# A written VectorE order for the opening of the feed-forward stream, and ordering edges behind ScalarE's copies of partial sums in the second layer

## The chip, the cores and the metric

One core of a Trainium2 chip runs the whole kernel in one launch. The metric is device time in microseconds, the median of several executions. TensorE (PE) multiplies, VectorE (DVE), ScalarE (ACT) and GpSimd (POOL) work element by element, SyncE (SP) issues the transfers. Each engine takes its instructions strictly in the order in which they stand in its queue; engines wait for one another by semaphores.

## The reference, cut to what matters

Two layers run over 1024 latent tokens and 256 context tokens. The change touches only the second half of a layer, the feed-forward block with a hidden width of 2816:

```
h2 = rms_norm(xl, norm_ffn) * (1 + sc2) + sh2
xl = xl + g2 * ((silu(h2 @ w_gate) * (h2 @ w_up)) @ w_down)
```

The first layer does this for the context tokens too (`has_ctx` in the kernel), the second for the latent tokens alone. Every float32 operand of a matrix product is split into two float16 parts, a high and a low one, and each product is the sum of three float16 products (high·high, high·low, low·high).

## The kernel before

The hidden width is cut into 22 columns of 128. Columns 0 and 1 are computed plainly, in what is called the opening here: `first_ffn` and the lines behind `wod()` multiply their gate and up weights with `h2` into the PSUM tiles `Sg` and `Su` (and `Sg1`, `Su1` for the first 512 tokens of column 1), ACT applies Silu into `sg`, and DVE multiplies `Su` into it. Those matmuls stand at L1415 and L466.

The other columns go in pairs through the stream (`steps`, from L1673). Each job is one weight block (gate, up or down) of 2x2 pieces times an activation block of 2x2 pieces, done with seven products instead of eight. The products are named "1" to "7"; each is 12 matmuls of 128x512 in a gate or up job and 6 in a down job, all at L1910. Product "1" uses piece B11 of the activations, "2" B21, "3" B22, "4" T4, "5" T1, "6" T2, "7" T3. B11 and B21 are parts of `h2` itself. T1, T2 and T3 are sums and differences of its blocks, which `h_ops` (L1518) makes once for each layer: for each of four slices k, three additions of high and low parts into tiles `rb` (two on POOL, one on DVE), three subtractions on DVE, one subtraction into the scratch `scv` from which T4 comes, and three splits into the tiles `tq` (high part on ACT, low part on DVE). In the first layer products "c0", "c1" and "c2" (L1922, PSUM tile `dx`) multiply the context tokens.

On the weight side POOL forms sums `ws` of staged blocks (`st`, `raw`), and `piece_ahead` (L1716) splits the pieces into the tile `hlp`, ACT the high part and DVE the low one. There is room for four pieces of a gate or up job ahead of PE.

Each job owns three PSUM banks, `Swb`, `Swc` and `Swa`; two sets take turns. Bank b takes product "1", then "6", "5" and "3" on top. After "1", "6" and "5" the running sum has to be taken out before the next one may be added, which `copy` (L1808) does on ACT, into one of four parts of `scv` (named `T` in the profile). `consume` (L1820) does what follows each product, and puts later work into `late` with a step number (`defer`, L1814), which `run_late` (L1925) runs after that step. `t_ops` (L1576) turns two finished columns into the seven operands of the next down job.

The written order of these calls sets a priority; a scheduler then places each instruction on its engine's queue, and may let one pass another where nothing binds them. Before the first product of the stream the tiles `Sg` and `Su` have to be read, since `split_banks` gives their PSUM to the stream's banks.

All activations are issued by one helper (L152), scalar_tensor_tensor by another (L166), tensor_tensor by a third (L169). In the changed kernel these lines are L175, L96 and L195 (every DVE operation has L96 there).

Of the kernel before, what the change touches and what calls it, by code (L numbers as in the profile page):

```python
# [81 lines left out]
def hybrid_kernel(ctx: ExitStack, tc: tile.TileContext, I, out, dbg=None):  # L82
    nc = tc.nc
    V, S, G, TE, DMA = nc.vector, nc.scalar, nc.gpsimd, nc.tensor, nc.sync
# [51 lines left out]
    order = mybir.DependencyInfo(mybir.DependencyClass.NoSync, mybir.DependencyReason.DATA)  # L136
# [12 lines left out]
    def act(o, i, f=AF.Copy, **kw):  # L149
        if f in (AF.Exp, AF.Ln) and tabs["kind"] != "el":  # L150
            preload()
        b = S.activation(o, i, f, **kw).ins  # L152
        if f in (AF.Exp, AF.Ln):
            after(b, tabs["pre"])
            tabs["last"] = tabs["last"][-7:] + [b]
        elif f in (AF.Tanh, AF.Silu):
# [6 lines left out]
            tabs["last"] = [b]  # L163

# [576 lines left out]
    for l in range(DEPTH):  # L741
# [776 lines left out]
        def h_ops():  # L1518
# [20 lines left out]
        wod()  # L1539
        wt = w_get(("gate", l, 1)), w_get(("up", l, 1), False)  # L1540
        sgs = [pt_((P, NTOK), F32, "pf", PFB, "sg") for _ in range(2)]
        pre = [bank("Sg1"), bank("Su1")]

        for k in range(4):
            tt(scv[:, k], h2[:, 4 + k, 0, H0], h2[:, 4 + k, 1, H0], ADD, G)
        for t0 in (512, 768):
            drain(nt[t0])
            for w, S_ in ((f0["wg"], f0["Sg"]), (f0["wu"], f0["Su"])):
                for _ in fm_steps(S_[:, t0:t0 + 256], w, h2, t0, 256):
                    pass  # L1550
                pump(2)
        sg, Sg, Su = sgs[0], f0.pop("Sg"), f0.pop("Su")
        f0.clear()
        act(sg[:, :NTq], Sg[:, :NTq], AF.Silu, scale=INV)
        stt(sg[:, :NTq], Su[:, :NTq], 1.0 / SW, sg[:, :NTq], MUL, MUL)
        spawn(h_ops())
        for w, S_ in zip(wt, pre):
            for _ in fm_steps(S_, w, h2, 0, 512):
                pump()
        act(sgs[1][:, H0], pre[0], AF.Silu, scale=INV)  # L1560
        stt(sgs[1][:, H0], pre[1], 1.0 / SW, sgs[1][:, H0], MUL, MUL)
        pre = None
        sg, Sg, Su = sgs[1], bank3("Sg"), bank3("Su")
        for w, S_ in zip(wt, (Sg, Su)):
            for (t0, n) in blks[1:]:
                fm(S_[:, t0:t0 + n], w, h2, t0, n)
                pump()
# [447 lines left out]
```

## Time and profile before

| | us |
|---|---|
| median of 3 executions | 2798.6 (2792.37 to 2801.43) |
| the profiled execution | 2797.35 |
| its span, first to last instruction | 2795.6 |
| opening of the first layer's stream | about 718 to 762 |
| first layer's stream | 762 to 1485 and a little beyond |
| opening of the second layer's stream | about 2144 to 2191 |
| second layer's stream | 2191 to 2752 |

Times in the rows are microseconds from the span's start. A row of the timeline has start, length, engine, line, operation, output and inputs, count, and in brackets how long the engine had been idle before it and whose end released it. A row of the groups has the count, the busy time, the mean in ns and the idle time before with its releasers. PE is the engine that is nearly always busy, so only its gaps, and what ended them, are time that can be had.

### The profile page before, as it was taken

What the parts mean: (1) busy time and instruction counts of PE and PEld (TensorE: products, weight loads), DVE (VectorE), ACT (ScalarE), POOL (GpSimd) and SP (SyncE); (2) the same over time, 40 slices, a digit from 0 to 9 for tenths busy, and PEclk for the clock granted to TensorE, in tenths of its full rate; (3) what the DMA queues carried; (4) which work ended last, traced back from release to release, by engine and by line L of the source; (5) the groups of instructions that cost most, each with busy time, mean ns of one, the idle gap of its engine ahead of it and who ended that gap; (6) DMA issues with size and microseconds to landing.
All of it is one profiled execution on the core that took longest, in us unless ns stands there. A gap on an engine that the chain in (4) does not pass through costs nothing. (4 is left out here: it accounts for less than half of the span.)

```text
span 2795.6 us, 53695 instructions
## 1 busy us (share of the span) xinstructions
PE 2568.2 (92%) x21403; PEld 1504.1 (54%) x21403; DVE 1882.3 (67%) x3217; ACT 1388.2 (50%) x2650; POOL 1283.8 (46%) x979
## 2 busy tenths in 40 slices
PE   7999989987799999999999998988878799999997
PEld 4875556655455555555555674545555344444444
DVE  5458867778756655656566558866788667576666
ACT  5345557775443434434344445466764444444353
POOL 1124446774434434444443213456764555555641
PEclk9999999999899999999999999999989899999999
DMA  9544499995123222232212222499982121211211
GB/s 299 143 122 113 127 203 186 196 178 116 52 84 91 77 90 83 85 90 77 69 38 78 69 62 69 122 187 180 194 172 69 46 61 53 61 54 53 61 53 76
DMA packets 631632, 296.23 MB, mean 106 GB/s; under 512 B 362888, under 2 KB 620756, under 8 KB 630868
## 3 DMA queue, kind: packets, MB, share of 16 engines
q1 hardware_dynamic: 631204, 292.73, 42.9%
q8 instruction: 167, 2.74, 0.4%
q14 instruction: 85, 0.70, 0.1%
q10 hardware_dynamic: 176, 0.07, 0.0%
HBM read 176.19 MB, written 20.87 MB: 70 GB/s over the span
## 5 line engine op out<-in xcount | busy, mean ns | idle before, releaser
L1910 PEld LDWEIGHTS <-hlp 128*128 128x128 f16 x5040 | 492.4, 98 | 607.5 <-issue 32.8
L1910 PE MATMUL Swb<-T,hlp 128*128 128x512 f16 x1920 | 445.2, 382 | 29.7 <-ACT T L152 14.0
L169 POOL TENSOR_TENSOR phl<-pf,phl 128x1280 f16<-128x1280 f32 (+1 forms) x132 | 345.3, 2618 | 173.7 <-ACT phl L152 115.8
L166 DVE SCALAR_TENSOR_TENSOR hlp<-ws,hlp 128x512 f16<-128x512 f32 (+1 forms) x320 | 231.5, 730 | 146.8 <-ACT hlp L152 119.8
L152 ACT ACTIVATE hlp<-ws 128x512 f16<-128x512 f32 (+1 forms) x320 | 163.6, 518 | 221.8 <-PE Swb L1910 89.3
L152 ACT ACTIVATE pf<-Sp,mx,rq 128x1280 f32<-128x1280 f32 (+1 forms) x144 | 189.6, 1318 | 117.2 <-DVE mx L1320 101.0
L1315 DVE TENSOR_REDUCE mx<-Sp 128x1 f32<-128x1280 f32 (+1 forms) x132 | 194.9, 1477 | 64.3 <-PE Sp L1311 57.2
L1910 PE MATMUL Swc<-T,hlp 128*128 128x512 f16 x960 | 227.2, 379 | 0.0
L1910 PE MATMUL Swb<-tq,hlp 128*128 128x512 f16 x960 | 220.5, 379 | 3.7 <-ACT T L152 3.7
L1374 PE MATMUL pwo<-T,hl 128*128 128x512 f16 (+1 forms) x960 | 194.0, 353 | 32.2 <-DVE X L166 14.4
L466 PE MATMUL pfm<-T,hl 128*128 128x512 f16 (+1 forms) x1032 | 218.1, 365 | 2.6 <-ACT E L152 2.4
L152 ACT ACTIVATE T<-sg 128x512 f16<-128x512 f32 (+1 forms) x170 | 100.3, 600 | 233.4 <-POOL sg L169 155.6
L1311 PE MATMUL Sp<-T 128*128 128x512 f16 (+1 forms) x800 | 171.3, 351 | 41.9 <-ACT pf L152 39.4
L166 DVE SCALAR_TENSOR_TENSOR hlp<-st,hlp 128x256 f16<-128x256 f32 (+1 forms) x201 | 144.2, 721 | 89.0 <-ACT hlp L152 74.1
L169 POOL TENSOR_TENSOR ws<-st 128x256 f32<-128x256 f32 (+1 forms) x97 | 103.9, 1079 | 185.0 <-DMA st<-in_w_ffn_down_dram 70.1
L1922 PE MATMUL dx<-T,hlp 128*128 128x256 f16 x1440 | 178.1, 273 | 11.4 <-DVE hlp L166 6.4
L169 POOL TENSOR_TENSOR X<-X,T 128x512 f32<-128x512 f32 x80 | 112.7, 1408 | 147.0 <-DVE X L166 110.6
L1910 PE MATMUL Swa<-T,hlp 128*128 128x512 f16 x720 | 169.1, 380 | 0.0
L1922 PEld LDWEIGHTS <-hlp 128*128 128x128 f16 x1440 | 139.4, 100 | 43.9 <-issue 9.9
L152 ACT ACTIVATE hlp<-st 128x256 f16<-128x256 f32 (+1 forms) x201 | 101.2, 510 | 110.8 <-PE Swb L1910 72.4
L1374 PEld LDWEIGHTS <-hl 128*128 128x128 f16 x960 | 97.6, 103 | 107.3 <-issue 37.1
L152 ACT ACTIVATE phl<-pf 128x1280 f16<-128x1280 f32 (+1 forms) x115 | 144.5, 1261 | 21.0 <-DMA pT<-phl 18.8
(322 smaller groups left out, 4742.3 us busy)
## 6 DMA issues: line engine op xcount, KB each, us to landing
T<-in_w_ada_dram SPq DMA_DIRECT2D x48, 512.0 KB
rawa<-in_w_ada_dram SPq DMA_DIRECT2D x48, 512.0 KB
st<-in_w_in_dram SPq DMA_DIRECT2D x32, 512.0 KB
st<-in_w_out_dram SPq DMA_DIRECT2D x64, 256.0 KB
st<-in_w_ffn_gate_dram SPq DMA_DIRECT2D x32, 512.0 KB
st<-in_w_ffn_up_dram SPq DMA_DIRECT2D x30, 512.0 KB
st<-in_w_ffn_down_dram SPq DMA_DIRECT2D x30, 512.0 KB
xs<-X SPq DMA_DIRECT2D x4, 2048.0 KB
```

What stands on the lines that cost most here:

```text
L152: b = S.activation(o, i, f, **kw).ins
L166: V.scalar_tensor_tensor(o, a, s, b, op0=o0, op1=o1)
L169: (e or V).tensor_tensor(o, a, b, op=op)
L466: mm(o, w[:, a, k, :], h[:, k, b, t0:t0 + n], start=(k == 0 and j == 0), stop=(k == nk - 1 and j == 2))
L1311: mm(Sp[:, e * nk + b0:e * nk + b0 + m], ql, qkv[:, 4 + h // 4, a, k0 + b0:k0 + b0 + m], start=(a == 0), stop=(a == 1), skip_group_check=True)
L1315: r = V.tensor_reduce(mx[:, :ne], Sp[:, :n].rearrange("p (e k) -> p e k", e=ne), axis=AX.X, op=MAX)
L1374: mm(pb, w[:, a, k, :], mixT[:, k0 + k, b, t0:t0 + n], start=(k == 0 and j == 0), stop=(k == 3 and j == 2))
L1910: mm(o, w[:, a, k, :], B[:, b], start=(s in "172" and k == 0 and j == 0), stop=(k == kh(i) - 1 and j == 2), skip_group_check=True)
L1922: mm(dbank[i][:, r * 256:(r + 1) * 256], w[:, a, k, :], B[:, b], start=(first and k == 0 and j == 0), stop=(not first and k == kh(i) - 1 a ...
```

## The change

DVE gets a wrapper that, while it is switched on, ties each DVE instruction by an ordering edge to the one written before it. An edge of this kind is no semaphore: it binds the scheduler on one engine's queue. It is on from the multiplication of `Su` into the first `sg` until the operands of `h_ops` are made.

`h_ops` does all three additions on DVE, in another sequence, and puts the `scv` subtraction behind the splits. It is no longer one of the threads that are advanced between matmuls; its four slices are called at set places. The whole opening stands behind the definitions of the stream, and the first weight pieces (`prepare()`) are prepared in it, ahead of the last slices of `h_ops`.

The stream's first steps are reordered: "1", "2", "c0", "7", "6" in place of "7", "1", "2", "c0", "6" in the first layer; "1" and "2" of the first job, "1" of the second, then "7", "6", "5" in the second layer, where it was "1", "7", "6", "2", "5".

In the second layer every activation that is written after a copy of a partial sum is tied behind that copy. The copies get six scratch buffers there in place of four in rotation, each given back when its reader has been issued. Late work runs after steps "1", "7", "6" and "4" only, and that of "4" in the same step.

```diff
-    V, S, G, TE, DMA = nc.vector, nc.scalar, nc.gpsimd, nc.tensor, nc.sync
+    row = {"on": False, "last": None}
+    class InRow:
...
+            def call(*a, **k):
+                b = f(*a, **k)
+                if row["on"]:
+                    if row["last"] is not None:
+                        tc.add_manual_dep(b.ins, row["last"].name, order, reason="written order")
+                    row["last"] = b.ins
+                return b
...
+    V = InRow(nc.vector)
...
         b = S.activation(o, i, f, **kw).ins
+        if tabs.get("copy") is not None:
+            tc.add_manual_dep(b, tabs["copy"].name, order, reason="behind the last copy")
...
-                for r, kk, c, e in ((r12, k, H1, G), (r11, k, H0, V), (r22, 4 + k, H1, G)):
-                    tt(r, h2[:, kk, 0, c], h2[:, kk, 1, c], ADD, e)
+                for r, kk, c in ((r22, 4 + k, H1), (r12, k, H1), (r11, k, H0)):
+                    tt(r, h2[:, kk, 0, c], h2[:, kk, 1, c], ADD)
...
-                tt(scv[:, k], scv[:, k], r22, SUB)
                 for op, r in (("T3", r12), ("T2", r22), ("T1", r11)):
                     split2(tpc[op][k], r, V)
+                tt(scv[:, k], scv[:, k], r22, SUB)
...
-            add(0, "7", "1", "2", "c0", "6")
+            add(0, "1", "2", "c0", "7", "6")
...
-            for i in range(nj + 1):
-                add(i, "1", "7")
...
+            add(0, "1", "2")
+            add(1, "1")
+            add(0, "7", "6", "5")
+            for i in range(1, nj + 1):
+                add(i, *("17" if i > 1 else "7"))
...
+        act(sg[:, :NTq], Sg[:, :NTq], AF.Silu, scale=INV)
+        in_row(True)
+        stt(sg[:, :NTq], Su[:, :NTq], 1.0 / SW, sg[:, :NTq], MUL, MUL)
+
+        ho = h_ops()
...
+        act(sg[:, 512:NTq], Sg[:, 512:NTq], AF.Silu, scale=INV)
+        if not last:
+            next(ho)
+        stt(sg[:, 512:NTq], Su[:, 512:NTq], 1.0 / SW, sg[:, 512:NTq], MUL, MUL)
...
+        prepare()
+        for _ in ho:
+            pass
+        drain()
+        in_row(False)
...
+        scs = [scv[:, i] for i in range(4)]
+        if not has_ctx:
+            scs += [T2v[:, o:o + 1024].bitcast(F32) for o in (7168, 15360)]
...
+            b = act(scs[z], src, scale=scale)
+            if not has_ctx:
+                tabs["copy"] = b
...
+                soon = n + (1 if has_ctx or s != "4" else 0)
...
-                    defer(n + 1, fn)
+                    defer(soon, fn)
...
-            run_late(n)
+
+            if has_ctx or s in "1764":
+                run_late(n)
```

What this does to the queues is shown at three places. The first is DVE's queue at the second layer's opening, from the end of the norm (`t`, and `T_72`, which is `h2`); `rb` and `tq` are the tiles of `h_ops`, `T_73` the scratch and the operands of the down jobs. Before:

```order
L166 SCALAR_TENSOR_TENSOR t<-X,prm_142,sq 128x256 x2
L169 TENSOR_TENSOR rb<-T_72 128x512
L166 SCALAR_TENSOR_TENSOR T_72<-t,prm_142,T_72 128x256 x2
L169 TENSOR_TENSOR rb<-rb 128x512
L169 TENSOR_TENSOR rb<-T_72 128x512
L169 TENSOR_TENSOR rb<-rb 128x512 x3
L166 SCALAR_TENSOR_TENSOR sg<-Su,sg 128x1024
L169 TENSOR_TENSOR T_73<-T_73,rb 128x512
L169 TENSOR_TENSOR tq<-rb,tq 128x512 x3
```

The same stretch of DVE's queue in the changed kernel:

```order
L96 SCALAR_TENSOR_TENSOR t<-X,prm_142,sq 128x256 x2
L96 SCALAR_TENSOR_TENSOR T_72<-t,prm_142,T_72 128x256 x2
L96 SCALAR_TENSOR_TENSOR sg<-Su,sg 128x1024
L96 TENSOR_TENSOR rb<-T_72 128x512 x3
L96 TENSOR_TENSOR sg<-sg 128x512
L96 TENSOR_TENSOR rb<-rb 128x512 x2
L96 TENSOR_TENSOR T_73<-sg,T_73 128x512
L96 TENSOR_TENSOR rb<-rb 128x512
L96 TENSOR_TENSOR tq<-rb,tq 128x512 x3
L96 TENSOR_TENSOR T_73<-T_73,rb 128x512
L96 SCALAR_TENSOR_TENSOR sg<-Su_26223,sg 128x512
```

The last writes of `h2` and the read of `Su` now stand ahead of all `rb` work. The read of the last `Su` (`sg<-Su,sg 128x512`) stood behind all four slices of `h_ops`; it now stands behind the second slice, ahead of the third, in the first layer behind the third (`128x768`). POOL's eight `rb<-T_72` additions in each layer are gone from its queue.

The second place is ACT's queue in the second layer's opening; `sg<-Sg` is a Silu, `hlp` a weight piece, `raw` one of the staged weight blocks. Before:

```order
L152 ACTIVATE sg<-Sg 128x1024
L152 ACTIVATE tq<-rb 128x512 x4
L152 ACTIVATE sg<-Sg_26222 128x512
L152 ACTIVATE T_73<-sg 128x512
L152 ACTIVATE hlp<-st 128x512 x2
L152 ACTIVATE tq<-rb 128x512 x6
L152 ACTIVATE hlp<-ws 128x512
L152 ACTIVATE sg<-Sg 128x512
```

The same stretch of ACT's queue in the changed kernel:

```order
L175 ACTIVATE sg<-Sg 128x1024
L175 ACTIVATE hlp<-st 128x512 x2
L175 ACTIVATE T_73<-sg 128x512
L175 ACTIVATE sg<-Sg_26222 128x512
L175 ACTIVATE T_73<-sg 128x512
L175 ACTIVATE tq<-rb 128x512 x3
L175 ACTIVATE hlp<-raw 128x512
L175 ACTIVATE T_73<-sg 128x512
L175 ACTIVATE hlp<-ws 128x512
L175 ACTIVATE tq<-rb 128x512 x2
L175 ACTIVATE sg<-Sg 128x512
L175 ACTIVATE tq<-rb 128x512
```

Three weight pieces moved forward, and one of them, `hlp<-raw`, now stands ahead of the second slice's `tq` and of the last Silu.

The third place is ACT's queue in the second layer's stream, where the first gate job after an up job ends; `T_73<-Swb` is the copy of a partial sum, `T_73<-sg` a split of `t_ops`, `sg<-sg` a Silu. Before:

```order
L152 ACTIVATE hlp<-ws 128x512
L152 ACTIVATE T_73<-sg 128x512
L152 ACTIVATE sg<-sg 128x512
L152 ACTIVATE hlp<-ws 128x512
L152 ACTIVATE T_73<-Swb 128x512
L152 ACTIVATE sg<-sg 128x512
L152 ACTIVATE hlp<-raw 128x512
L152 ACTIVATE T_73<-Swb 128x512
```

The same stretch in the changed kernel:

```order
L175 ACTIVATE hlp<-ws 128x512
L175 ACTIVATE T_73<-sg 128x512
L175 ACTIVATE T_73<-Swb 128x512
L175 ACTIVATE hlp<-ws 128x512
L175 ACTIVATE T_73<-Swb 128x512
L175 ACTIVATE sg<-sg 128x512 x2
L175 ACTIVATE hlp<-raw 128x512
```

Both Silus and one weight piece moved behind the copies; the split of `t_ops` still stands ahead of the first.

## Rows read from the trace of the kernel before

**Rows 1.** Busy time by stretch: stretch, length, PE, PEld, DVE, ACT, POOL, PEclk, DMA, GB/s.

```profile
718.00:762.00 44.00, 29.99 (x178) 16.80 (x177) 39.63 (x49) 18.23 (x32) 25.34 (x16) 0.87 0.13 37
762.00:1485.00 723.00, 723.00 (x4707) 402.26 (x4706) 434.28 (x659) 299.56 (x604) 311.63 (x269) 1.00 0.26 77
2144.00:2191.00 47.00, 28.18 (x122) 12.31 (x120) 42.19 (x50) 19.59 (x33) 26.77 (x17) 0.78 0.11 34
2191.00:2752.00 561.00, 544.08 (x2504) 245.26 (x2504) 366.54 (x529) 252.77 (x491) 297.15 (x251) 1.00 0.18 54
```

**Rows 2.** Who waited for whom, PE, 718 to 762: us, times, longest.

```profile
PE Sg L1415 <- DVE T L166: 2.6, 2, 1.8
```

**Rows 3.** Timeline of PE in the first layer's opening.

```profile
740.11 7.96 PE L466 MATMUL Su<-T,hlr 128*128 128x512 f16 x48
...
760.63 1.46 PE L1922 MATMUL dx<-T,hlp 128*128 128x256 f16 x6 [6.43 <-DVE hlp L166]
761.88 3.79 PE L1910 MATMUL Swc<-tq,hlp 128*128 128x512 f16 x12
...
772.43 2.75 PE L1910 MATMUL Swb<-tq,hlp 128*128 128x512 f16 x12
```

**Rows 4.** Timeline of PE in the second layer's opening.

```profile
2162.24 5.34 PE L466 MATMUL Su<-T,hlr 128*128 128x512 f16 x24
2181.37 1.01 PE L1910 MATMUL Swb<-T,hlp 128*128 128x512 f16 x2 [13.79 <-DVE sg L166]
...
2185.89 4.45 PE L1910 MATMUL Swb<-T,hlp 128*128 128x512 f16 x10 [1.80 <-DVE hlp L166]
2191.18 0.59 PE L1910 MATMUL Swb<-tq,hlp 128*128 128x512 f16 x2 [0.84 <-ACT T L152]
...
2195.92 2.32 PE L1910 MATMUL Swa<-T,hlp 128*128 128x512 f16 x10
2198.08 2.75 PE L1910 MATMUL Swb<-tq,hlp 128*128 128x512 f16 x12
```

**Rows 5.** Timeline of DVE, POOL and ACT in both openings.

```profile
722.72 1.24 ACT L152 ACTIVATE sg<-Sg 128x1280 f32<-128x1280 f32 x1 [2.77 <-PE Sg L1415]
...
724.34 2.48 DVE L169 TENSOR_TENSOR rb<-rb 128x512 f32<-128x512 f32 x4
...
726.75 1.48 DVE L166 SCALAR_TENSOR_TENSOR sg<-Su,sg 128x1280 f32<-128x1280 f32 x1
...
2143.36 4.18 POOL L169 TENSOR_TENSOR rb<-T 128x512 f32<-128x512 f16 x3
...
2143.61 1.64 DVE L169 TENSOR_TENSOR rb<-T 128x512 f32<-128x512 f16 x1
```

**Rows 6.** Timeline of SP and POOL: two weight transfers and one use.

```profile
2162.43 0.37 SPq L370 DMA_DIRECT2D raw<-in_w_ffn_up_dram  x1
...
2185.89 0.37 SPq L370 DMA_DIRECT2D st<-in_w_ffn_up_dram  x1
...
2189.71 1.46 POOL L169 TENSOR_TENSOR ws<-raw,st 128x512 f32<-128x512 f32 x1 [6.24 <-DMA st<-in_w_ffn_up_dram]
```

**Rows 7.** Groups of PE in 2191 to 2752, the two with idle time.

```profile
L1910 PE MATMUL Swb<-T,hlp 128*128 128x512 f16 x948 | 219.3, 381 | 13.9 <-ACT T L152 13.8
...
L1910 PE MATMUL Swb<-tq,hlp 128*128 128x512 f16 x480 | 110.3, 379 | 3.7 <-ACT T L152 3.7
```

**Rows 8.** Timeline of PE: two of the stops of that stream.

```profile
2318.40 2.75 PE L1910 MATMUL Swb<-T,hlp 128*128 128x512 f16 x12 [2.57 <-ACT T L152]
...
2467.87 4.05 PE L1910 MATMUL Swb<-T,hlp 128*128 128x512 f16 x18 [2.24 <-ACT T L152]
```

**Rows 9.** Timeline of ACT ahead of the first of these stops.

```profile
2316.12 0.63 ACT L152 ACTIVATE T<-sg 128x512 f16<-128x512 f32 x1 [2.52 <-DVE sg L169]
...
2316.72 0.63 ACT L152 ACTIVATE sg<-sg 128x512 f32<-128x512 f32 x1
...
2317.77 0.58 ACT L152 ACTIVATE T<-Swb 128x512 f32<-128x512 f32 x1
```

More of the change, by code (lines that the diff above doesn't have):

```diff
@@ L1595, in hybrid_kernel @@
-        if has_ctx:
-            for e in range(2):
-                split2(a_ctx(0, e), sgs[e][:, T:], G)
-        for which in ("C11", "C22", "C12", "C21"):
-            t_ops(0, which)
-        hlt = [wk.tile([P, 2048], F16, tag="hl", name="hlp", bufs=2) for _ in range(2)]
+        hlt = []
         ring = [None] * 8
@@ L1783, in free @@
                     ring[s] = None
+        wod()
+        wt = w_get(("gate", l, 1)), w_get(("up", l, 1), False)
+        sgs = [pt_((P, NTOK), F32, "pf", PFB, "sg") for _ in range(2)]
+        pre = [bank("Sg1"), bank("Su1")]
+        for k in range(4):
+            tt(scv[:, k], h2[:, 4 + k, 0, H0], h2[:, 4 + k, 1, H0], ADD, G)
+        for t0 in (512, 768):
+            drain(nt[t0])
+            for w, S_ in ((f0["wg"], f0["Sg"]), (f0["wu"], f0["Su"])):
+                for _ in fm_steps(S_[:, t0:t0 + 256], w, h2, t0, 256):
+                    pass
+                pump(2)
@@ new lines, in hybrid_kernel, with t_ops @@
+        prepare()
+        for _ in ho:
+            pass
+        drain()
+        in_row(False)
+        for k in range(4):
+            split2(h2[:, k, :, H1], scv[:, k], V)
+        def t_ops(p, which):
+            (p11, p12), (p21, p22) = ((s[:, H0], s[:, H1]) for s in sgs)
+            if which == "C11":
+                split2(a_op(p, "B11"), p11, G)
+            elif which == "C22":
+                split2(a_op(p, "B22"), p22, G)
+            elif which == "C12":
+                tt(p11, p12, p11, SUB)
+                tt(p12, p22, p12, SUB)
+                tt(p22, p22, p11, SUB)
+                split2(a_op(p, "T3"), p12, V)
+                split2(a_op(p, "T2"), p22, V)
+                split2(a_op(p, "T1"), p11, V)
+            else:
+                split2(a_op(p, "B21"), p21, G)
+                tt(p21, p21, p22, SUB)
+                split2(a_op(p, "T4"), p21, V)
@@ L1786, in hybrid_kernel @@
+        if has_ctx:
+            for e in range(2):
+                split2(a_ctx(0, e), sgs[e][:, T:], G)
+        for which in ("C11", "C22", "C12", "C21"):
+            t_ops(0, which)
         adaq = list(range(48)) if l == 0 else []
@@ L1864, in consume @@
                     tt(dst, src, t, ADD)
-                    defer(n + 1, lambda: act(dst, dst, AF.Silu, scale=INV))
+                    end()
+                    defer(soon, lambda: act(dst, dst, AF.Silu, scale=INV))
                 else:
@@ L1870, in fn @@
                         tt(dst, dst, t, MUL, G)
+                        end()
                         if fin:
@@ L1946, in hybrid_kernel @@
         run_late(len(steps) + 9)
+        tabs["copy"] = None
         while pend or adaq:
```

107 lines of the change are left out of this document (40 added, 67 removed).

## The prediction

> **What bounds the kernel now.** I read the busy times by stretch first: PE's row says where time can be had. In the first layer's stream PE is busy for all of its 723.0 us, so nothing done to other engines there shortens it, and whatever the opening ahead of it saves is kept to the end. PE is idle in three stretches that the change touches: 14.0 us of the 44 in the first opening, 18.8 of the 47 in the second, 16.9 of the 561 in the second layer's stream [rows 1]. Together 49.7 us, 1.8%: no more than that, and a little for the clock, can be won. Then the waits and the timeline of PE, for what ends each gap. The first opening has two waits, 2.6 us in all, for DVE's last writes of `h2` [rows 2], and two further gaps behind the matmuls of the last `Su`, the second of 6.4 us up to 761.9 [rows 3]. The second has the same 2.6 us (the pattern repeats) and 13.8 us until DVE has read `Su` [rows 4]. In both, the granted clock over the stretch is below full, 0.87 and 0.78 [rows 1]. Directly after the 13.8 us PE works at the lower level, 1.2 GHz: ten matmuls take 4.45 us there, and ten start within 2.16 us, 0.216 each, later [rows 4]. In the stream every wait is for one thing, ACT's copy of bank b: 13.8 us in front of the products with operand `T` and 3.7 in front of those with `tq` [rows 7]. I call such a wait a stop; there are nine of the first sort and four of the second.
>
> **Price of a DVE instruction in the openings.** Four 128x512 subtractions take 2.48 us, 0.62 each. An addition that runs while POOL runs takes 1.64, so a meeting costs 1.0 [rows 5]. Both engines then read SBUF. The Trainium skill, "SBUF — State Buffer", section "SBUF: two separate sides", says that DVE and GpSimd hold a shared port pair exclusively for a whole instruction and the loser waits fully. By it a meeting could cost a whole POOL addition, 1.4 us, and the gains of both openings below would be some 2 us smaller each; the measured row has less, and I take it.
>
> **`h2` ahead of `rb`, twice.** The two last writes of `h2` leave the place behind an `rb` addition. Two writes of 128x256 are shorter than two 0.62 operations, and PE has other matmuls for that long, so both waits go and PE ends its opening 2.6 us earlier: at 745.5 in the first layer (748.07 before, [rows 3]) and at 2165.0 in the second (2167.58, [rows 4]). This is inside the next two sums.
>
> **First opening.** The stream may begin when DVE has read the last `Su`. The first Silu starts 2.6 us earlier, at 720.1, and takes 1.24; DVE's multiplication takes 1.48 [rows 5], so at 722.9 DVE begins the rest. By the new order 35 instructions of 128x512 stand ahead of the read: 35 x 0.62 = 21.7, and 0.9 for the read of 768 columns (between the 0.62 of 512 and the 1.48 of 1280): 745.5, just where PE is done. That is the lower end. Upwards come meetings with POOL, which loses its eight additions but still has about eight instructions there (splits and weight sums), 1.0 each, and one hand-over (DVE to ACT to POOL and back) that I price at 2 to 3 us from the 2.5 us waits for such chains [rows 9]: 756 at the worst. I take the middle, 751. Products "1", "2" and "c0" need nothing of `h_ops`, then comes "7": 36 matmuls at 0.216 and 24 of half that width, 10.4, and 1.5 for the clock (twelve matmuls after the old gap took 3.79 us, where 2.6 is their full pace [rows 3]): 762.9. The last slice's T3 must be there by then: 14 more DVE instructions after the read, 8.7, and a meeting or two: 761, not late. Before, the same products were done at 772.4 [rows 3]. **Gain 9.5 us**; 15 at the lower end. At the upper one T3 comes at about 768 and 4 are left.
>
> **Second opening.** Here the new order puts a transfer in the way. The `raw` weights may be fetched when PE has left the gate weights; this was at 2162.4 and will be at 2159.8, and a block arrives 3.8 us after its issue (2185.89 to 2189.71) [rows 6]: 2163.6. ACT's split of it stands ahead of the second slice's `tq` and of the last Silu, so behind this one instruction eight others wait, and DVE for them. Nine ACT instructions at 0.52 (two in 1.05 us, [rows 9]) end at 2168.3, then three on DVE, with a meeting or two: PE starts at about 2172, where it was 2181.4. The fetch itself was hidden before and is not now. Three products need nothing of `h_ops`, then "7": 48 x 0.216 = 10.4 and 2.6 for the clock after a gap of 7 us would end at 2185. But the last two slices are still to come: 28 DVE instructions up to the last T3, 17.4, and three or four meetings: 2191.5, then the last three matmuls: 2192. Before, 48 matmuls were done at 2198.1 [rows 4]. **Gain 6 us**; 13 if T3 does not bind, none if it comes 6 us later still.
>
> **The copies.** At the first stop in the rows ACT did a split, a Silu and a weight piece and then the copy at 2317.77 [rows 9], which let PE go on [rows 8]. In the new order the Silu and the weight piece stand behind the copy, the split still ahead. The copy comes earlier by 2317.77 - 2316.72 = 1.05, and three stops of this sort shrink by that. The six other `T` stops (the one of 2.24 stands for them [rows 8]) lose one weight piece of about 0.52 ahead of their copy. Together 6.3 of the 13.8 [rows 7]. Of the `tq` stops one, 0.84, belongs to the opening [rows 4]; at the other three only weight pieces that are ready stand ahead now, and 2.9 us go. **Gain 9.2 us**, between nothing (new stops of the same sort) and all 16.7. What stays late is the split itself, which waits for DVE and POOL.
>
> **Sum.** 9.5 + 6 + 9.2 = 24.7. The profiled execution took 2797.35, 1.25 less than the median of 2798.6 (2792.37 to 2801.43); so 2772.65 by its own time and 2774 as a median. The four scratch operations and the ada matmuls that change place cost nothing: their engines are idle for half of the stretch [rows 1].
>
> **Rivals.** *The openings win nothing.* DVE is busy for 39.6 of 44 and 42.2 of 47 us [rows 1]: it is the full engine there, it takes over eight additions in each layer (8 x 0.62 = 5.0), and with more meetings than I counted T3 arrives as late as PE did before. Against it: before, half of them were slowed by POOL. Only the copies gain: 2798.6 - 9.2 = 2789. *All goes through.* PE starts when its own opening ends, and no stop is left: 15 + 13 + 16.7 = 44.7, 2754. Against it stands the split ahead of the copy, and the fetch. *The edges hold ACT back.* Slower than before: each copy now bars ACT from all work written behind it until PE has ended the product copied. A weight piece used to slip ahead; now it may be late by a whole product, 2.6 us. Room for four pieces means it is needed three products after its place is free, 7.8 us, and its split takes about 1.3; so it decides from a delay of more than 6 us, two products, on. If it struck each of the 20 gate and up jobs for 2 us, 40 would be lost against 15.5 won: 2823. For it: ACT is the only engine for both. Against it: ACT is busy for 252.8 of 561 us [rows 1], and no PE wait in the stream is for a piece [rows 7]. *The edges do not bind.* Chains through POOL and DVE set the copies and DVE's load the openings; 4 us remain: 2795.
>
> **How the numbers follow.** The forecast has 0.55, the openings without gain 0.17, all through 0.12, the slower case 0.07, no effect 0.09. A measurement of this kernel can tell some 0.3%, 8.4 us, so faster means below 2790.2. The forecast's cases, all through, and a bit over half of the case at 2789 make faster 0.77; the rest of that and the case of no effect make same 0.16; slower 0.07. Bounds of the unknown prices: 2755 (15, 12 and 16.7 saved) to 2795 (4 and nothing else). Eight times in ten I expect it between 2757 and 2792.
>
> **What would show it.** Right: in the changed profile PE waits no more for DVE's `T` writes in the openings; the first stream product starts near 749 and near 2170 with a gap of under 8 us ahead, and in the second opening a further gap stands ahead of the last `tq` product; ACT shows a wait of some 9 us for the `raw` transfer; the sum of PE's waits for ACT in the second stream is about 7 us. Wrong: PE waiting for `hlp` in the stream (the slower rival), a gap in the first opening as long as before with DVE full (the first rival), or an unchanged 17 us of waits for copies, with the splits of `t_ops` directly ahead of each.

## The result and the profile after

The changed kernel takes 2774.6 us (median, 2772.4 to 2780.5) where the kernel before takes 2800.0 (2792.4 to 2803.3) on the same chip: a ratio of 0.9921, 95% interval 0.9907 to 0.9935. That is 22 us or 0.8% faster by the ratio. The forecast was 2774, range 2757 to 2792.

The profiled execution is the slowest of its six: 2780.47 us, span 2778.7. It is only 16.9 us shorter in span than the one of before: it takes 4.4 us longer ahead of the openings and between them, where nothing was changed (3.3 us ahead of the first, 1.1 in the first layer's stream and the second layer's attention). So stages are compared from a mark of their own, not from the span's start.

Busy time by stretch of the kernel after (columns as in [rows 1]):

```profile
718.00:762.00 44.00, 34.15 (x195) 19.24 (x194) 39.75 (x53) 20.13 (x34) 16.46 (x12) 0.88 0.08 25
...
2144.00:2191.00 47.00, 35.95 (x152) 15.41 (x151) 42.02 (x56) 19.53 (x34) 13.91 (x9) 0.85 0.08 23
2191.00:2752.00 561.00, 552.18 (x2567) 251.01 (x2566) 392.17 (x550) 253.67 (x502) 311.38 (x252) 1.00 0.17 55
```

PE's idle time fell from 14.0 to 9.9 us in the first opening and from 18.8 to 11.1 in the second; DVE is as busy as before in both (39.8 and 42.0 us), POOL less (16.5 and 13.9, where [rows 1] has 25.3 and 26.8). Now the waits, PE in the second layer from 2150 to 2760 (engine, line, awaited, line: us in total, times, longest):

```profile
PE Swb L1960 <- ACT T L175: 5.3, 10, 1.5
PE Swb L1960 <- DVE hlp L96: 4.6, 1, 4.6
PE Swb L1960 <- DVE sg L96: 4.0, 1, 4.0
PE Swb L1960 <- ACT hlp L175: 3.2, 2, 2.5
PE pdn L2009 <- DVE X L96: 2.2, 2, 1.3
```

The 17.5 us of waits for ACT's copies [rows 7] are 5.3. The single gap of 13.8 us ahead of the stream [rows 4] is 4.0, but two waits for `hlp`, the weight pieces, have come behind it. The timeline of PE in both openings of the kernel after:

```profile
724.11 2.32 PE L1441 MATMUL Sg<-T,hlr 128*128 128x512 f16 x10
...
756.48 1.03 PE L1960 MATMUL Swb<-T,hlp 128*128 128x512 f16 x2 [9.05 <-DVE sg L96]
...
765.80 2.75 PE L1960 MATMUL Swc<-tq,hlp 128*128 128x512 f16 x12
768.49 0.64 PE L509 MATMUL pada<-rawa,csp 128*32 128x128 f32 x16
...
773.42 1.26 PE L1972 MATMUL dx<-T,hlp 128*128 128x256 f16 x10 [1.02 <-DVE hlp L96]
...
2167.71 1.01 PE L1960 MATMUL Swb<-T,hlp 128*128 128x512 f16 x2 [3.98 <-DVE sg L96]
...
2182.76 0.60 PE L1960 MATMUL Swb<-tq,hlp 128*128 128x512 f16 x2 [2.51 <-ACT hlp L175]
2187.93 0.61 PE L1960 MATMUL Swb<-tq,hlp 128*128 128x512 f16 x1 [4.56 <-DVE hlp L96]
```

There is no wait for DVE's `T` ahead of these rows any more. In the first opening one gap of 9.05 us stands where two of 5.0 and 6.4 stood [rows 3].

**A measure for an opening.** Single gaps only show where PE stood still. I therefore take the time from the first matmul on the last block of `h2` (the row `Sg<-T,hl` x1 at 713.77 and 2139.07 of before, at 717.07 and 2137.97 of after) to the end of the 240th product matmul of full width, counted along the timeline with two `dx` matmuls of 256 columns for one. The changed kernel, the openings run and the edges-only run below have the same opening code and give 98.2, 98.1, 98.1 for the first and 96.6, 98.3, 95.6 for the second; before and the stream's run (e2) share the old opening and give 103.6 and 105.0, 100.6 and 100.5. So differences of 1.4 us in the first and 2.7 in the second mean nothing. Differences are taken before rounding.

| kernel | first | second | sum | ratio to before (interval) |
|---|---|---|---|---|
| before | 103.6 | 100.6 | 204.2 | 1 |
| after | 98.2 | 96.6 | 194.8 | 0.9921 (0.9907 to 0.9935) |
| openings alone (e1) | 98.1 | 98.3 | 196.4 | 0.9978 (0.9965 to 0.9990) |
| stream alone (e2) | 105.0 | 100.5 | 205.5 | 0.9952 (0.9936 to 0.9968) |
| edges, early release (e4) | 98.1 | 95.6 | 193.7 | 0.9941 (0.9924 to 0.9957) |
| T3 first (e10) | 99.6 | 99.9 | 199.5 | 0.9948 (0.9933 to 0.9962) |
| T3 first, pipelined (e11) | 99.6 | 97.0 | 196.6 | 0.9932 (0.9919 to 0.9946) |
| additions on POOL (e5) | 99.2 | 93.0 | 192.2 | 0.9912 (0.9899 to 0.9926) |
| no enforced order (e6) | 98.9 | 92.3 | 191.2 | 0.9910 (0.9897 to 0.9924) |
| old step order (e9) | 98.2 | 94.0 | 192.2 | 0.9913 (0.9900 to 0.9927) |
| these three undone (e12) | 106.6 | 96.5 | 203.1 | 0.9950 (0.9934 to 0.9966) |
| no order, additions on POOL (e13) | 105.7 | 96.8 | 202.5 | 0.9952 (0.9937 to 0.9966) |
| three undone, late pieces (e14) | 104.1 | 101.7 | 205.8 | 0.9954 (0.9940 to 0.9969) |
| late pieces (e15) | 102.3 | 98.8 | 201.1 | 0.9948 (0.9931 to 0.9965) |

By this measure the change gains 5.5 us in the first opening (103.62 to 98.16) and 4.0 in the second. The 5.5 us are kept through the first layer's stream: its first `pdn` matmul (1502.25 before, 1500.09 after) stands 788.5 and 783.0 us behind the mark. From the first matmul of the first down job (2236.93 before, 2231.82 after) to the first `pdn` matmul (2752.13, 2733.53) the second layer's stream gains 13.5 (515.2 to 501.7). The end behind it is 1.7 longer (43.5 to 45.2). Together that is 21 us, where the ratio gives 22 and the medians 25.4.

### The profile page after: what moved, and what is told of

Same layout as the page of the kernel before. It is cut to its first block, busy times and chain, and to the rows that moved or that the text cites. A ratio compares the mean times of both kernels' runs of the same rounds, so it can differ in the third digit from the quotient of the medians.

```text
span 2778.7 us, 53623 instructions
## 1 busy us (share of the span) xinstructions
PE 2564.7 (92%) x21403; PEld 1500.9 (54%) x21403; DVE 1890.2 (68%) x3233; ACT 1387.1 (50%) x2650; POOL 1269.3 (46%) x963
## 5 line engine op out<-in xcount | busy, mean ns | idle before, releaser
L175 ACT ACTIVATE pf<-Sp,mx,rq 128x1280 f32<-128x1280 f32 (+1 forms) x144 | 189.6, 1317 | 118.1 <-DVE mx L96 98.8
L175 ACT ACTIVATE T<-sg 128x512 f16<-128x512 f32 (+1 forms) x170 | 98.8, 599 | 165.0 <-POOL sg L195 96.3
L195 POOL TENSOR_TENSOR sg<-sg,T 128x512 f32<-128x512 f32 x60 | 88.7, 1478 | 143.6 <-DVE T L96 143.2
```

Source lines behind the costliest of these rows:

```text
L195: (e or V).tensor_tensor(o, a, b, op=op)
```

## Experiments: the two halves

**Openings alone (e1).** The stream's part is undone:

```diff
             b = act(scs[z], src, scale=scale)
-            if not has_ctx:
-                tabs["copy"] = b
...
-                soon = n + (1 if has_ctx or s != "4" else 0)
+                soon = n + 1
...
-            if has_ctx or s in "1764":
-                run_late(n)
+            run_late(n)
```

> The new openings without the stream's part: no edge behind the copies and partial-sum work released after every product, as before; six scratch places and the new step order stay. Theory (two independent parts; the openings are worth 5.5 + 4 = 9.5 us by the two traces, the stream's part 13.5): 2800 - 9.5 = 2790.5, ratio 0.9966; PE's waits for ACT's copies in the second layer's stream are back at 15 to 19 us, and its start of the first pdn product comes 13 us later than in the changed kernel. Rival A (the openings win nothing that is kept, all is the stream's): ratio 0.999 to 1.001. Rival B (the new openings and step order bring nearly all, the edges nothing): 2775, ratio 0.991, waits for copies near 5 us.

Measured: 0.9978, 6 us, and the waits for copies are back to the full sum, so the six scratch places alone take none away (PE's waits, 2232 to 2770):

```profile
PE Swb L1958 <- ACT T L175: 17.5, 13, 2.4
```

So 3 to 10 us of the openings are kept to the end; the theory's 0.9966 is inside the interval, rival A's 0.999 stands at its edge, and rival B is outside.

**The stream alone (e2).** The opening's code, `h_ops` and the step order are those of before; edges, scratch and release are the changed kernel's. Against the kernel before:

```diff
+        if tabs.get("copy") is not None:
+            tc.add_manual_dep(b, tabs["copy"].name, order, reason="behind the last copy")
...
+        if not has_ctx:
+            scs += [T2v[:, o:o + 1024].bitcast(F32) for o in (7168, 15360)]
...
-            run_late(n)
+            if has_ctx or s in "1764":
+                run_late(n)
```

> The stream's part alone: edges, six scratch places and the later release of partial-sum work as in the changed kernel, but the opening's code and the step order of the kernel before. Theory (independent parts): 2800 - 13.5 = 2786.5, ratio 0.9952; PE's gaps in the openings are as before (6.4 and 13.8 us, and 2.6 for DVE's h2 writes in each), its waits for ACT's copies in the second stream are 4 to 8 us. Rival A (the edges act only with the new step order): ratio 0.998 to 1.000 and waits for copies of 12 us or more. Rival B (the stream's part is all): ratio 0.991.

Measured: 0.9952, the value forecast by the theory. The openings take 105.0 and 100.5 us, as before within the spread, and the waits for copies are those of the changed kernel (PE's waits, 2232 to 2770):

```profile
PE Swb L1948 <- ACT T L175: 5.0, 9, 1.7
```

The gains of the two halves, 0.22% and 0.48%, add up to 0.70%, beside 0.79% for both together: they are independent within the intervals.

**Edges without the later release (e4).** The edges stay, the release is that of before:

```diff
-                soon = n + (1 if has_ctx or s != "4" else 0)
+                soon = n + 1
...
-            if has_ctx or s in "1764":
-                run_late(n)
+            run_late(n)
```

> The changed kernel with its ordering edges, but partial-sum work is released after every product, one product later for the last one, as before. The split of the weighted partial sum then stands ahead of a copy again, where the prediction left it. Theory (the prediction's own sum for the edges: 17.5 us of waits less 9.2): waits for copies of 8 to 9 us, time 3 us above the changed kernel, 2778, ratio 0.992. Rival A (the edges alone do it all): waits of 5 us, 2775. Rival B (without the later release the edges bring nothing): waits of 14 us or more, 2785, ratio 0.9945.

Measured: PE's waits for copies from the first down job (2226.49) to the first `pdn` (2731.24) are 8.0 us; in the same stage before has 16.7 and after 5.0.

```profile
PE Swb L1960 <- ACT T L175: 8.0, 9, 2.8
```

The edges alone take away 8.7 us of waits, the later release 3.0 more. The stream's length says the same: 515.2 before, 504.8 with the edges alone, 501.7 with both (501.5 to 502.2 in the eleven kernels that have both). The forecast of 8 to 9 us of waits came true; by the ratios the time lies 5.6 us above the changed kernel for the 3 expected, but the two intervals overlap, and that the release is worth 3 us is carried by the traces alone.

## Experiments: which part of the new opening counts

**T3 of all slices first (e10).** My reading of the two traces was that DVE's work ahead of the read of the last `Su`, and then ahead of the last T3, sets both openings. So the order inside `h_ops` was turned round, with one loop over the slices for T3, one for T2 and one for T1:

```diff
-                tt(r11, r12, r11, SUB)
-                tt(r12, r22, r12, SUB)
-                tt(r22, r22, r11, SUB)
-                for op, r in (("T3", r12), ("T2", r22), ("T1", r11)):
-                    split2(tpc[op][k], r, V)
...
+                tt(r22, r22, r12, SUB)
+                split2(tpc["T3"][k], r22, V)
+                yield
...
+                tt(r22, r22, r11, ADD)
+                split2(tpc["T2"][k], r22, V)
...
+            for k, r12, r11 in held:
+                tt(r12, r12, r11, SUB)
+                split2(tpc["T1"][k], r12, V)
```

> The openings again, with h_ops turned round: T3 of all four slices first (sums kept in the unused half of T2), the read of the last Su behind them, then T2 of all, then T1. Theory (what sets both openings is DVE's work ahead of the last Su's read and of the last slice's T3): in the first the read comes 6 us earlier, PE starts near 750 instead of 756.5 and goes through; in the second PE starts 2 us earlier and its further stops (2.5 and 4.6 us) go: about 6 + 8 = 14 us under the changed kernel, 2761, ratio 0.986. Rival A (the weight pieces and ACT's splits set it: POOL's sums and the hlp pieces come no earlier): only the first read is won and PE stops for hlp afterwards, 3 us under the changed kernel, 2772. Rival B (DVE's whole work sets it, its order does not matter): same as the changed kernel, 2775.

Measured: 0.9948, 7.6 us slower than the changed kernel by the ratios; the two intervals just touch. The first step came out as forecast, and the gain was lost a few products later. Timeline of PE:

```profile
749.38 0.60 PE L1972 MATMUL Swb<-T,hlp 128*128 128x512 f16 x2 [0.83 <-DVE sg L96]
...
760.47 1.45 PE L1972 MATMUL Swb<-tq,hlp 128*128 128x512 f16 x6 [0.74 <-ACT T L175]
...
764.11 0.38 PE L1972 MATMUL Swb<-tq,hlp 128*128 128x512 f16 x1 [1.97 <-ACT tq L175]
...
2185.15 1.03 PE L1972 MATMUL Swb<-tq,hlp 128*128 128x512 f16 x2 [7.65 <-ACT hlp L175]
```

PE starts 33 us behind the mark instead of 39 and runs at full pace through four products. Then it stops for T2, for weight pieces, for T2 again, up to 780. The 240th matmul comes 1.4 us later than in the changed kernel, in the second opening 3.3. My reading was that no order makes the operands of the fifth and sixth product come earlier than DVE can write them; but DVE was not full here, as the next run takes up.

**The same, pipelined (e11).** DVE had idled in that run for ACT's halves (0.69 us, three times in each opening) and for the last `Su` (3.5 us); and then it had worked on the first down operands ahead of T2. Here the subtraction of each split is written one slice later, T2 of one or two slices stands ahead of the read, and the down operands behind T1 (`low` is the DVE half of a split; `rest` holds T1 and the down operands, and stands behind the first product in the second layer).

```diff
+                act(tpc["T3"][k][:, 0], r22)
+                if k:
+                    low("T3", k - 1, rs[2 * k - 2])
...
-        for _ in ho:
-            pass
+        for _ in range(3 if last else 2):
+            next(ho)
         drain()
-        in_row(False)
...
+            for which in ("C11", "C22", "C12", "C21"):
+                t_ops(0, which)
+            in_row(False)
...
+            if n == 0 and not has_ctx:
+                rest()
```

> The run with T3 first lost its early start again: DVE idled 3.5 us ahead of the read of the last Su and 0.7 us four times behind a fresh ACT half, and then did some twenty subtractions for the first down products (needed 60 us later) between the T2 and T1 pieces that PE waited for. Here the same work is put so that no instruction follows the ACT half that it needs directly, T2 of one or two slices stands ahead of the read, T1 of all stands ahead of the work for the down products, and in the second layer the S2 weight piece stands ahead of T1. Theory (DVE's order decides, what is urgent first): PE starts near 749.5 in the first opening and loses at most 3 us to a late weight piece, in the second it starts near 2166 on the changed kernel's clock and the stops of 2.5 and 4.6 us go: 12 us under the changed kernel, 2763, ratio 0.987. Rival A (DVE's whole work up to the fifth product sets it, whatever the order): within 3 us of the changed kernel, 2775, ratio 0.991. Rival B (the chain through ACT and the weight pieces): slower than the changed kernel by 5 us or more as the run before.

Measured: 0.9932, between 3 us slower than the changed kernel and level with it. PE:

```profile
751.58 0.59 PE L1992 MATMUL Swb<-T,hlp 128*128 128x512 f16 x2 [1.25 <-DVE sg L96]
...
767.20 0.59 PE L515 MATMUL pada<-sel,sa 128*128 128x2 f32 x2 [3.79 <-ACT sa L175]
...
2183.98 3.73 PE L1992 MATMUL Swb<-tq,hlp 128*128 128x512 f16 x10 [2.80 <-DVE hlp L96]
2191.40 1.03 PE L1992 MATMUL Swc<-tq,hlp 128*128 128x512 f16 x2 [3.70 <-ACT hlp L175]
```

Again the head start is 8 us (31.4 behind the mark), and again it goes: to an ACT copy of the ada product that now stands behind the splits, and to weight pieces. The 240th matmul stands at 99.6 and 97.0, no earlier than in the changed kernel. With this my theory, that the order of `h_ops` is what is to be had, had fallen. So the parts of the opening were undone one by one.

**Two of three additions back on POOL (e5).**

```diff
-                for r, kk, c in ((r22, 4 + k, H1), (r12, k, H1), (r11, k, H0)):
-                    tt(r, h2[:, kk, 0, c], h2[:, kk, 1, c], ADD)
+                for r, kk, c, e in ((r22, 4 + k, H1, G), (r12, k, H1, G), (r11, k, H0, V)):
+                    tt(r, h2[:, kk, 0, c], h2[:, kk, 1, c], ADD, e)
```

> The changed kernel with two of the three rb additions of every slice back on POOL (eight in each opening), all else the same. Theory (DVE's work sets both openings and a POOL addition beside it costs DVE 1.0 us, more than the 0.62 that it saves): 8 x 0.38 = 3 us slower in each opening, 6 us over the changed kernel, 2781, ratio 0.993; PE's first stream product starts 2 to 3 us later in both. Rival A (POOL's help is nearly free since DVE does other work meanwhile): 3 to 5 us faster in each, 2767, ratio 0.988. Rival B (the chain matters, each slice waits for POOL's two additions of 1.4 us with DVE idle): 10 us or more slower in each opening, 2797, the whole gain of the openings gone.

**No enforced order on DVE (e6).**

```diff
-        in_row(True)
```

> The changed kernel without the enforced order on DVE in the openings: same code, but the scheduler places DVE's instructions. It puts the read of the last Su some 16 instructions later in the first opening and some 20 later in the second, behind h_ops and weight pieces; the additions stay on DVE. Theory (what the last T3 waits for is the amount of DVE work, and three products that need no T3 fill PE in either order; a read 10 us later just removes their head start): 3 to 4 us lost in each opening, 7 us over the changed kernel, 2782, ratio 0.9935. Rival A (the enforced order is the whole gain of the openings): 10 us over, 2785 or more. Rival B (the order brings nothing, the new step order and the additions do): 2775.

**The step order of before (e9).**

```diff
-            add(0, "1", "2", "c0", "7", "6")
+            add(0, "7", "1", "2", "c0", "6")
```

and, in the second layer, the loop of before in place of the new one.

> The changed kernel with the step order of before: product 7, which needs T3 of all four slices, first again, instead of two or three products that need nothing of h_ops. Theory (the early products are what fills PE until the last T3): PE's gap ahead of the stream grows from 9 to 18 us in the first opening and from 4 to 15 or more in the second, 7 to 8 us lost in each after what PE makes up, 2790, ratio 0.9965: about what the stream's part alone leaves plus 3. Rival (the enforced order and the additions make the gain, the step order matters little): 2775 to 2779.

Measured: 0.9912, 0.9910 and 0.9913. My theory was wrong in all three: none of the parts is missed when it alone is undone. PE's gaps move and their sum hardly changes (from the mark to the 240th matmul, both openings: 23.2, 22.8 and 24.0 us, 24.2 in the changed kernel); the rows are of e5, e6 and e9, in this order:

```profile
755.61 1.04 PE L1960 MATMUL Swb<-T,hlp 128*128 128x512 f16 x2 [8.96 <-DVE sg L96]
...
2180.82 0.58 PE L1960 MATMUL Swc<-tq,hlp 128*128 128x512 f16 x1 [3.42 <-ACT tq L175]
```

```profile
752.51 4.67 PE L1959 MATMUL Swb<-T,hlp 128*128 128x512 f16 x12 [10.82 <-DVE sg L96]
...
2165.49 4.73 PE L1959 MATMUL Swb<-T,hlp 128*128 128x512 f16 x12 [6.05 <-ACT tq L175]
```

```profile
752.09 1.01 PE L1959 MATMUL Swc<-tq,hlp 128*128 128x512 f16 x2 [9.26 <-DVE sg L96]
...
2182.59 0.58 PE L1959 MATMUL Swc<-tq,hlp 128*128 128x512 f16 x1 [5.49 <-ACT tq L175]
```

Which engine does the additions matters little: with eight of them back on POOL the first opening is 1.0 us longer, inside the spread of the measure, and the second 3.6 shorter. In all three runs the second opening (92.3 to 94.0 us) is shorter than in every run of the changed code (95.6 to 98.3); each of these values is one trace.

**Several undone at once (e12, e13).** e12 undoes all three, e13 the enforced order and the additions, with the hunks above.

> The openings with all three parts undone together that cost nothing when undone one by one: no enforced order on DVE, two rb additions of each slice on POOL, the step order of before. What stays of the new opening is where it is written: h_ops is no longer fed in between PE's products, and the first weight pieces are prepared ahead of the last slices. Theory (that the pieces and h_ops are written where they are is the gain; each of the three parts only moves PE's idle time about): PE's idle time in both openings together stays at 22 to 26 us (24 in the changed kernel, 34 before), 2775, ratio 0.9915. Rival A (any one of the three suffices, so undoing one shows nothing): idle time 32 us or more, 2784, ratio 0.995, as the stream's part alone.

> No enforced order and the two additions back on POOL, with the new step order: the two undone parts that measured best alone, together. Theory (as in the run with three parts undone): idle time of 22 to 24 us, 2772, ratio 0.9905, the best of the versions or level with them. Rival A (redundant parts): idle time near 28 us, 2779, ratio 0.993.

Measured: 0.9950 and 0.9952, as the stream alone. The theory fell and rival A held: 8 to 9 us are lost (e13's interval is clear of the changed kernel's, e12's touches it), and already with two of the three undone, so the parts stand in for each other. By the measure the whole loss lies in the first opening, which takes 106.6 and 105.7 us for 98.2; the second keeps its gain (96.5 and 96.8 for 96.6). What is back in the first is PE's waits ahead of the opening's end, and the long gap. Timeline of PE in e13:

```profile
724.34 0.49 PE L1441 MATMUL Sg<-T,hl 128*128 128x256 f16 x3 [1.66 <-DVE T L96]
725.63 0.39 PE L1441 MATMUL Sg<-T,hl 128*128 128x256 f16 x2 [0.80 <-DVE T L96]
...
765.86 4.91 PE L1959 MATMUL Swb<-T,hlp 128*128 128x512 f16 x12 [13.06 <-DVE sg L96]
```

and of DVE, where the first row is an `h_ops` addition and the second holds the last two writes of `h2`:

```profile
721.36 1.64 DVE L96 TENSOR_TENSOR rb<-T 128x512 f32<-128x512 f16 x1
722.92 2.65 DVE L96 SCALAR_TENSOR_TENSOR T<-t,prm,T 128x256 f16<-128x256 f32 x2
```

The same place in e5 (row order kept, additions on POOL) and in e6 (no order, additions on DVE), one row of each:

```profile
719.32 2.66 DVE L96 SCALAR_TENSOR_TENSOR T<-t,prm,T 128x256 f16<-128x256 f32 x2
```

```profile
715.27 0.87 DVE L96 SCALAR_TENSOR_TENSOR T<-t,prm,T 128x256 f16<-128x256 f32 x2
```

Two things hold the `h2` writes up: an addition ahead of them on DVE, and POOL's additions beside them, which stretch two writes from 0.87 to 2.65 us. The enforced order removes the first; additions on DVE remove the second and shorten the first (0.68 instead of 1.64). One of the two is nearly enough, since PE has other matmuls for most of that time: it waits 1.3 us in e5, not at all in e6, and with neither 2.46, where before has 2.57. Up to its last `Su` PE then needs 34.5 us from the mark for 30.1 in the changed kernel, the clock included. The rest of e13's loss is the longer gap behind it, 13.06 us for 9.05, which the later read of the last `Su` ends; that this read is late because of the slowed start of `h_ops` I infer from the order of these rows and did not test. In the second opening the same two waits are back and PE starts the stream 12 us later than in the changed kernel; but behind the start it stops there for 0.7 us where the changed kernel stops for 8.5, and at the 240th matmul the two are level. In the first the changed kernel stops only for 1.0 behind the start, so there is nothing to make the loss up with.

**The first weight pieces late (e15, e14).** e15 is the changed kernel, e14 the run with three parts undone, both with the first `prepare()` back behind `h_ops` and the splits of the down operands:

```diff
         hlt += [wk.tile([P, 2048], F16, tag="hl", name="hlp", bufs=2) for _ in range(2)]
-        prepare()
         for _ in ho:
             pass
```

> The changed kernel with only this undone: the first weight pieces are prepared behind h_ops and the splits again. Theory (early pieces count): PE waits for hlp pieces behind the read of the last Su, idle time of the openings grows by 5 us or more, 2781, ratio 0.9935. Rival (the scheduler places the pieces well in either case): 2775, ratio 0.9915.

> As the run with three parts undone, and the first weight pieces are also prepared behind h_ops and the splits of the first down operands again, as before. Theory (the early pieces are the part that counts): the gain of the openings is gone, idle time 32 us or more, 2784, ratio 0.995. Rival (it is that h_ops is not fed in between PE's products, with the h2 writes ahead of it): no change against the run with three parts undone, 2775, ratio 0.9915.

Measured: e15 0.9948, its interval touching that of the changed kernel only at the edge: 7.6 us by the ratios, and by the measure 4.2 in the first opening and 2.2, inside the spread, in the second. e14 0.9954, no change against e12 in time: by the measure its first opening is 2.5 us shorter and its second 5.1 longer. As e12 had lost the gain already, e14 decides nothing between its theory and its rival. PE in e15:

```profile
753.35 5.30 PE L1959 MATMUL Swb<-T,hlp 128*128 128x512 f16 x12 [3.34 <-DVE sg L96]
...
765.39 0.59 PE L1959 MATMUL Swb<-tq,hlp 128*128 128x512 f16 x2 [2.65 <-ACT T L175]
...
769.86 1.03 PE L1959 MATMUL Swc<-tq,hlp 128*128 128x512 f16 x2 [2.97 <-ACT hlp L175]
```

The idle sum up to the 240th matmul is that of the changed kernel (10.6 us for 10.9; the expected growth of 5 us did not come), but three stops of some 3 us stand in place of one of 9, and much of what lies between them runs at the lower clock: 12 matmuls in 5.30 us, 0.44 each, which is the 1.2 GHz level. The 240th matmul is 4.2 us late. From 755 to 775 PE did this in the changed kernel and in e15 (stretch, length, PE busy and count, granted clock):

```profile
755.00:775.00 20.00, 17.50 (x104) 0.87 0.11 30
```

```profile
755.00:775.00 20.00, 13.57 (x57) 0.67 0.09 27
```

## Why the prediction was right, point by point

**The outcome.** 2774.6 for 2774, faster by more than the measurement's 0.3%. The three gains have the forecast signs and a sum of 23.0 where 24.7 was forecast, of which the end takes 1.7 back; but the split is 5.5, 4.0 and 13.5 where it was 9.5, 6 and 9.2. Two terms too high and one too low nearly cancelled: the ways of the gains were foreseen, but that the total came so near is luck.

**`h2` ahead of `rb`: right, and a little more.** Both waits for DVE's `T` are gone. From the mark to its last `Su` PE needs 30.1 us instead of 34.3, 4.2 less for the 2.6 forecast; the rest is the clock, for behind the old waits ten matmuls took 3.75 us and now 2.32, as the first row of the timeline after shows. What the prediction did not see: with the additions on DVE the waits go without the enforced order too (e6).

**First opening: term too large, 9.5 for 5.5, inside its bounds of 4 and 15.** On the clock of before the stream starts at 753.2 (756.48 - 3.3), where 751 was taken from between 745.5 and 756, and the last T3 lands 3 us later than the 761 forecast (764, just in time). From that start to the end of "7" the 11.9 us forecast were 12.0, so 7.2 us of the 9.5 are left there. Another 1.8 go until the 240th matmul, 1.0 in a stop for a weight piece and 0.6 in a block of ada matmuls. "The ada matmuls that change place cost nothing" was wrong: before, PE did this block in its long gap, in the changed kernel it stands behind "7" (768.49 in the rows above). Timeline of PE, before:

```profile
748.00 0.65 PE L483 MATMUL pada<-rawa,csp 128*32 128x128 f32 x16
```

The misread step is in [rows 3]: the 6.4 us gap is ended by DVE's `hlp`, a weight piece, and at 760.6, not 761.9. I priced it as part of a wait for the read of `Su` and counted DVE instructions only, and never priced that `prepare()` moves ahead of the last slices. e15 shows that the openings' gain needs this move: undone alone, it takes 7.6 us of time, and no other part undone alone takes any.

**Second opening: the size near, 4.0 for 6, by a mechanism that did not occur.** The step that failed is the `raw` fetch. I left its issue tied to PE's leaving of the gate weights [rows 6], 2.6 us earlier. SP issued it 25 us earlier still (timeline of SP, after):

```profile
2134.60 0.50 SPq L396 DMA_DIRECT2D raw<-in_w_ffn_up_dram  x1
```

ACT never waited for it. It is the same move of `prepare()`: in the other runs with early pieces the fetch is issued at 2128 to 2140, in those with late ones (before, e2, e14, e15) at 2156 to 2163. So the stream started 4 us behind PE's own end instead of 7, and 12.6 us earlier behind the mark than before (29.7 for 42.3). Most of that head start was given back in two stops for the `S2` piece, 2.5 and 4.6 us. POOL's sum for it takes its tile from the buffers that `rb` uses, and waited until DVE was done with the third slice (timeline of POOL, after):

```profile
2180.49 1.56 POOL L195 TENSOR_TENSOR ws<-ws,st 128x512 f32<-128x512 f32 x1 [10.72 <-DVE tq L96]
```

DVE's half of the piece, at 2187.2, then stood behind the fourth slice's additions. That the last T3 binds near 2191.5 came out well: it lands at 2189.1, on the clock of before 2190.2.

**The copies: mechanism right, size 13.5 for 9.2.** The term was a sum of work that goes behind the copy, 9.2 us of waits; e4 has exactly this part and loses 8.7 us of waits, 10.4 us in length. At the first stop the Silu of [rows 9] no longer stands between the split and the copy (timeline of ACT, after):

```profile
2309.56 0.63 ACT L175 ACTIVATE T<-sg 128x512 f16<-128x512 f32 x1 [2.52 <-DVE sg L96]
2310.09 0.58 ACT L175 ACTIVATE T<-Swb 128x512 f32<-128x512 f32 x1
```

The stop that this ends is 0.42 us, for 2.57 in [rows 8]. What was mis-sized is "what stays late is the split itself": the later release in the code moves part of that too, 3.0 us of waits, 3.1 in length. I had priced it at nothing.

**What was not in the sum.** The end is 1.7 us longer: PE's `pdn` waits for DVE's `X` are 2.2 us where they were 0.9. It shows in all kernels with the stream's part (44.6 to 45.2) and hardly without (43.5 and 44.1). That late partial sums finish behind the stream would explain it; no run tests this.

**The signs and the rivals.** On the clock of before the stream's first products start at 753.2 and 2168.8, where the sign said near 749 (the sum said 751) and 2170, with gaps of 9.05 and 3.98 us ahead for under 8; the waits for copies are 5.3 us for about 7; the 9 us wait of ACT for `raw` did not come. The openings without gain: refuted for the change as made by e1, though e13 shows that two undone parts are enough to lose it. Edges that hold ACT back: refuted, no wait for a piece stands in the stream behind the opening. Edges that do not bind: refuted by e4. All through: it needed no stop at all, and 17 us of waits for ACT and DVE are left in the second layer.

**Is there a better version?** None that the runs tell apart: e5, e6 and e9 measure 0.9910 to 0.9913, with intervals that overlap 0.9907 to 0.9935 over more than half of their width. e6 reaches this without the enforced order. Whether one of them is faster by the 2 to 3 us of the ratios, which their shorter second openings fit, stays open, as does what a better order for POOL's `S2` sum would give.

## What to carry to other kernels

Where an engine is full in a transition, turning its order round can move the bottleneck's wait without shortening the way to the last operand (e10, e11); look first for the few instructions that others wait for (here the `h2` writes and the first weight pieces and their fetch) and get them ahead. Read the releaser of every gap, not its length alone, and price each call that moves, the DMA it issues included. Undo parts in pairs as well as alone before calling one of them needless: two parts may each be enough.

## What the runs showed of the hardware

Nearly the same idle time cost PE more in e15, where it was cut in three, than in the changed kernel. Stops of 3.34, 2.65 and 2.97 us left the granted clock at 0.67 from 755 to 775, against 0.87 behind the one stop of 9.05 us, and the 240th matmul came 4.2 us later with the idle sum 0.3 us smaller. This is one pair of traces, and more stops did not always mean a lower clock: in e10 seven shorter ones, of 0.2 to 2.0 us, left 0.91 in the same stretch (columns as above):

```profile
755.00:775.00 20.00, 14.35 (x87) 0.91 0.19 53
```

DVE's two writes of 128x256 took 0.87 us alone and 2.65 beside POOL's additions, and an addition of 128x512 took 0.68 alone and 1.64. That is 0.9 to 1.0 us a meeting, whatever DVE's own instruction takes. Two of these meetings, POOL and DVE in the second opening of before:

```profile
2143.36 1.33 POOL L169 TENSOR_TENSOR rb<-T 128x512 f32<-128x512 f16 x1
2143.61 1.64 DVE L169 TENSOR_TENSOR rb<-T 128x512 f32<-128x512 f16 x1
...
2144.66 1.59 POOL L169 TENSOR_TENSOR rb<-T 128x512 f32<-128x512 f16 x1
2145.17 1.37 DVE L166 SCALAR_TENSOR_TENSOR T<-t,prm,T 128x256 f16<-128x256 f32 x1
```

DVE's addition ends 0.56 us behind the POOL addition that was under way, its write 0.29 us, both less than they take alone (0.68 and 0.47). The Trainium skill, "SBUF — State Buffer", section "SBUF: two separate sides", lets the loser wait for the whole instruction that holds the port. The trace agrees: DVE waits until POOL's instruction has ended. As it came 0.25 and 0.51 us after POOL's start, it paid less than a whole POOL addition of 1.4 us [rows 5]. And for the opening as a whole the additions on POOL cost nothing (e5), which no count of meetings had told.
